# Holding the first store of a streaming RMSNorm until the fifth chunk has been loaded

## Chip, cores and metric

One core of one Trainium2 chip. The metric is the device time of one execution in microseconds (us), median over runs.

## The reference

```python
# x: (16, 1024, 512) float32, gamma: 512 ones, eps = 1e-5
rms = np.sqrt(np.mean(x ** 2, axis=-1, keepdims=True) + eps)
return np.maximum(x / rms * gamma, 0).astype(np.float32)
```

x has 33.55 MB, and the result as many: 67.1 MB must pass between HBM and the core whatever the schedule.

## The kernel before

The 16384 rows are cut into 8 chunks of 4.19 MB (128 partitions x 16 rows x 512 values). SBUF holds 6 chunks ("slots"). A chunk is normalised in place, and its slot is stored from where it was loaded. Every large transfer, load or store, is issued by SyncE into one queue. ScalarE squares and sums half a chunk at a time; VectorE follows with reciprocal, scaling and maximum, and counts each finished half chunk in `done`. GpSimd waits for each load and passes the news on to ScalarE.

```python
loads = [(0, 0, G), (0, G, K - G)] + [(i, 0, K) for i in range(1, nchunks)]   # chunk 0 in two halves
...
def store(i):
    nc.sync.dma_start(out=ov[i], in_=slot_ap(i)).then_inc(sem_slot[i % nslots], 16)
...
for m, (i, a, r) in enumerate(loads):
    if i < nslots:                        # chunks 0 to 5: issued at once
        load(m)
nxt = nslots
for i in range(nchunks):
    nc.sync.wait_ge(done, per * (i + 1))  # per = 2 half chunks
    store(i)
    if i >= 1 and nxt < nchunks:          # chunks 6 and 7 reuse slots 0 and 1
        nc.sync.wait_ge(sem_slot[nxt % nslots], 32)   # its load and its store have landed
        ... load(nxt); nxt += 1
```

`sem_slot[s]` rises by 16 when a load into slot s has landed and by 16 more when its store has.

Of the kernel before, what the change touches and what calls it, by code (L numbers as in the profile page):

```python
# [12 lines left out]
@with_exitstack  # L13
def kernel(
    ctx: ExitStack,
    tc: tile.TileContext,
    x: bass.AP,
    gamma: bass.AP,
    eps: bass.AP,
    out: bass.AP,  # L20
):



    nc = tc.nc
    P = nc.NUM_PARTITIONS

    x2 = x.flatten_outer_dims()
    out2 = out.flatten_outer_dims()
    n, d = x2.shape  # L30
    rows = n // P
    inv_d = 1.0 / d
    K = 16
    G = 8
    nchunks = rows // K
    nslots = 6
    ngroups = rows // G
    per = K // G
    xv = x2.rearrange("(c p k) d -> c p k d", p=P, k=K)
    ov = out2.rearrange("(c p k) d -> c p k d", p=P, k=K)  # L40

    singles = ctx.enter_context(tc.tile_pool(name="singles", bufs=1))
    psum = ctx.enter_context(
        tc.tile_pool(name="psum", bufs=1, space=bass.MemoryType.PSUM))

    gseed = singles.tile([P, d], F32, name="gseed")
    gamma_sb = singles.tile([P, d], F32, name="gamma_sb")
    eps_sb = singles.tile([P, 1], F32, name="eps_sb")
    ss = singles.tile([P, rows], F32, name="ss")
    rms = singles.tile([P, rows], F32, name="rms")  # L50
    rstd = singles.tile([P, rows], F32, name="rstd")
    slots = singles.tile([P, nslots * K * d], F32, name="slots")
    junk = psum.tile([P, G, d], F32, name="junk")


    loads = [(0, 0, G), (0, G, K - G)] + [(i, 0, K) for i in range(1, nchunks)]


    sem_half = tc.alloc_semaphore("half")
    sem_slot = [tc.alloc_semaphore(f"slot{s}") for s in range(nslots)]  # L60
    sem_g = tc.alloc_semaphore("gam")
    sem_z = tc.alloc_semaphore("zero")
    ready = tc.alloc_semaphore("ready")
    sq = tc.alloc_semaphore("sq")
    done = tc.alloc_semaphore("done")
    sa = tc.alloc_semaphore("sa")
    sv = tc.alloc_semaphore("sv")

    def slot_ap(i):
        s = (i % nslots) * K * d  # L70
        return slots[:, s:s + K * d].rearrange("p (k d) -> p k d", d=d)

    def load(m):
        i, a, r = loads[m]
        nc.sync.dma_start(out=slot_ap(i)[:, a:a + r, :],
                          in_=xv[i][:, a:a + r, :]
                          ).then_inc(sem_half if m == 0 else sem_slot[i % nslots], 16)

    def loaded(engine, m):
        i = loads[m][0]  # L80
        if m == 0:
            engine.wait_ge(sem_half, 16)
        else:
            engine.wait_ge(sem_slot[i % nslots], 32 * (i // nslots) + 16)

    def store(i):
        nc.sync.dma_start(out=ov[i], in_=slot_ap(i)).then_inc(sem_slot[i % nslots], 16)

    ctx.enter_context(tc.manual_schedule(engines={mybir.EngineType.SP}))
    with tc.tile_critical():  # L90
        for m, (i, a, r) in enumerate(loads):
            if i < nslots:
                load(m)
        nxt = nslots
        for i in range(nchunks):
            nc.sync.wait_ge(done, per * (i + 1))
            store(i)
            if i >= 1 and nxt < nchunks:
                nc.sync.wait_ge(sem_slot[nxt % nslots], 32)
                for m, (c, a, r) in enumerate(loads):  # L100
                    if c == nxt:
                        load(m)
                nxt += 1

        for m, (i, a, r) in enumerate(loads):
            loaded(nc.gpsimd, m)
            nc.gpsimd.sem_inc(ready, r // G)

        nc.vector.memset(gseed, 0.0).then_inc(sem_z, 1)  # L109
        nc.vector.memset(eps_sb, eps).then_inc(sem_z, 1)  # L110

        nc.scalar.wait_ge(sem_z, 1)
        nc.scalar.dma_start(out=gseed[0:P:32, :],
                            in_=gamma[None, :].to_broadcast([P // 32, d])
                            ).then_inc(sem_g, 16)
        nc.scalar.preload_act_table(ACTF.Sqrt)  # L116
        nc.scalar.wait_ge(sem_z, 2)
        with nc.scalar.Fori(0, ngroups) as gi:
            nc.scalar.wait_ge(ready, 1)
            nc.scalar.sem_inc(ready, -1)  # L120
            base = nc.scalar.snap((gi % (nslots * per)) * (G * d))
            col = nc.scalar.snap(gi * G)
            for j in range(G):
                a = nc.scalar.activation(  # L124
                    out=junk[:, j, :], in_=slots[:, bass.ds(base + j * d, d)],
                    func=ACTF.Square, accum_out=ss[:, bass.ds(col + j, 1)])
                if j == G - 1:
                    a.then_inc(sa, 1)
            nc.scalar.wait_ge(sa, 1)
            nc.scalar.sem_inc(sa, -1)  # L130
            nc.scalar.activation(out=rms[:, bass.ds(col, G)], in_=ss[:, bass.ds(col, G)],  # L131
                                 func=ACTF.Sqrt, bias=eps_sb, scale=inv_d).then_inc(sq, 1)

        nc.vector.wait_ge(sem_g, 16)
        nc.vector.stream_shuffle(gamma_sb, gseed, [0] * 32)  # L135
        with nc.vector.Fori(0, ngroups) as gi:
            nc.vector.wait_ge(sq, 1)
            nc.vector.sem_inc(sq, -1)  # L138
            base = nc.vector.snap((gi % (nslots * per)) * (G * d))
            col = nc.vector.snap(gi * G)  # L140
            blk = slots[:, bass.ds(base, G * d)]
            nc.vector.reciprocal(out=rstd[:, bass.ds(col, G)],  # L142
                                 in_=rms[:, bass.ds(col, G)]).then_inc(sv, 1)
            nc.vector.wait_ge(sv, 1)
            nc.vector.sem_inc(sv, -1)  # L145
            for j in range(G):
                row = slots[:, bass.ds(base + j * d, d)]
                r = nc.vector.scalar_tensor_tensor(  # L148
                    out=row, in0=row, scalar=rstd[:, bass.ds(col + j, 1)], in1=gamma_sb,
                    op0=ALU.mult, op1=ALU.mult)  # L150
                if j == G - 1:
                    r.then_inc(sv, 1)
            nc.vector.wait_ge(sv, 1)
            nc.vector.sem_inc(sv, -1)  # L154
            nc.vector.tensor_scalar_max(out=blk, in0=blk, scalar1=0.0).then_inc(done, 1)  # L155

    with nc.sync.register("landed") as landed:
        nc.sync.reg_mov(landed, 32)
        for s in range(nchunks - nslots, nslots):
            nc.sync.wait_ge(sem_slot[s], landed)  # L160
        nc.sync.reg_mov(landed, 64)
        for s in range(nchunks - nslots):
            nc.sync.wait_ge(sem_slot[s], landed)
# [35 lines left out]
```

## Time and profile before

| | before |
|---|---|
| time, median of the first 3 runs | 162.84 us (162.69 to 162.90) |
| span of the profiled run | 160.9 us |
| moved | 67.12 MB, mean 417 GB/s |
| busiest compute engine | VectorE, 78% |
| bulk queue, share of the 16 DMA engines' time | 97.6% |
| first store issued, landed | 31.07, 72.1 us |
| last VectorE instruction ends, last store lands | 146.4, 159.9 us |

The row to read is the DMA row, not the compute rows: engines with 54 and 78% wait for something. The page's chain of the last work ends at VectorE's last instruction, so what fills the last 13 us has to be looked up in SyncE's waits and in the transfers' landings. In lines of the profile, SPq is SyncE's sequencer, DVE is VectorE, ACT ScalarE and POOL GpSimd. In what follows L4 is the load and S4 the store of chunk 4, counted from 0, so that the "fifth chunk" is chunk 4.

### The profile page before, as it was taken

The page shows a single profiled execution, that of the slowest core. Times are in us where ns is not written, and L with a number is a line of the kernel's source. Part 1 is how long each engine was busy: PE and PEld are TensorE (multiplying, and loading weights), DVE is VectorE, ACT ScalarE, POOL GpSimd, SP SyncE. Part 2 cuts the span into 40 slices and gives each one's busy share as a digit, 9 for nine tenths or more (in the row PEclk, how much of TensorE's full clock was granted, in tenths as well). Part 3 has the DMA queues.
Part 4 walks back from the last instruction along what each step waited for, and adds up shares of the span by engine and source line. Part 5 has one row for each costly group of instructions (what it writes and reads, how often), then busy time and mean ns, then how long its engine had stood idle before and what let it go on. Part 6 is the DMA issues. An engine that isn't in the chain of part 4 may idle for free. (4 is left out here: it accounts for less than half of the span.)

```text
span 160.9 us, 1006 instructions
## 1 busy us (share of the span) xinstructions
DVE 126.0 (78%) x164; ACT 86.3 (54%) x273; POOL 0.2 (0%) x4
## 2 busy tenths in 40 slices
DVE  1103989898989899999999999999999999994000
ACT  3088929889988988988900198503994000000000
POOL 0000000000000000000000000000000000000000
DMA  5999999999999998999999999999999999999993
GB/s 155 434 432 415 521 391 391 513 399 391 489 424 391 481 432 367 415 391 489 424 391 489 424 391 448 464 391 440 456 407 432 456 415 424 464 415 424 464 407 138
DMA packets 2456, 67.12 MB, mean 417 GB/s; under 512 B 276, under 2 KB 276, under 8 KB 280
## 3 DMA queue, kind: packets, MB, share of 16 engines
q1 hardware_dynamic: 2448, 67.11, 97.6%
q10 hardware_dynamic: 8, 0.01, 0.0%
HBM read 33.56 MB, written 33.55 MB: 417 GB/s over the span
## 5 line engine op out<-in xcount | busy, mean ns | idle before, releaser
L124 ACT ACTIVATE junk<-slots 128x512 f32 x128 | 74.5, 582 | 30.6 <-ACTq L120 30.3
L148 DVE SCALAR_TENSOR_TENSOR slots<-slots,rstd,gamma_sb 128x512 f32 x128 | 86.2, 747 | 4.8 <-DVEq L145 4.8
L155 DVE TENSOR_SCALAR slots<-slots x16 | 36.7, 2294 | 2.4 <-DVEq L154 0.2
L124 ACT ACTIVATION_READ_ACCUMULATOR junk<-slots x128 | 23.9, 187 | 0.0
L142 DVE RECIPROCAL rstd<-rms x16 | 3.1, 196 | 6.3 <-DVEq L138 6.3
L131 ACT ACTIVATE rms<-ss,eps_sb x16 | 4.8, 301 | 3.0 <-ACTq L130 3.0
L135 DVE LOAD_MASK_SELECT gamma_sb<-gseed x1 | 0.0, 14 | 5.8 <-DMA gseed<-in_gamma_dram 5.8
L116 ACT ACT_TABLE_LOAD x1 | 1.3, 1283 | 2.8 <-issue 2.8
L109 DVE MEMSET gseed<- 128x512 f32 x1 | 0.5, 485 | 1.1 <-SPq L90 1.1
L135 DVE STREAM_SHUFFLE gamma_sb<-gseed 128x512 f32<-128x512 f32 x1 | 0.7, 715 | 0.0
L180 POOL MEMSET const-bfloat16-1.0<- 128x1 bf16 x1 | 0.1, 103 | 0.0
L180 POOL MEMSET const-uint8-127<- 128x1 uint8 x1 | 0.1, 102 | 0.0
L180 POOL MEMSET const-float32-0.0<- 128x1 f32 x1 | 0.1, 100 | 0.2 <-issue 0.2
L180 POOL MEMSET const-float32-1.0<- 128x1 f32 x1 | 0.1, 99 | 0.0
L110 DVE MEMSET eps_sb<- 128x1 f32 x1 | 0.1, 59 | 0.0
## 6 DMA issues: line engine op xcount, KB each, us to landing
out_dram<-slots SPq DMA_DIRECT2D x8, 4096.0 KB, 31.3
slots<-in_x_dram SPq DMA_DIRECT2D x7, 4096.0 KB, 30.3
slots<-in_x_dram SPq DMA_DIRECT2D x2, 2048.0 KB, 9.6
gseed<-in_gamma_dram ACTq DMA_DIRECT2D x1, 8.0 KB
```

What stands on the lines that cost most here:

```text
L109: nc.vector.memset(gseed, 0.0).then_inc(sem_z, 1)
L110: nc.vector.memset(eps_sb, eps).then_inc(sem_z, 1)
L116: nc.scalar.preload_act_table(ACTF.Sqrt)
L124: a = nc.scalar.activation(out=junk[:, j, :], in_=slots[:, bass.ds(base + j * d, d)], func=ACTF.Square, accum_out=ss[:, bass.ds(col + j, 1)])
L131: nc.scalar.activation(out=rms[:, bass.ds(col, G)], in_=ss[:, bass.ds(col, G)], func=ACTF.Sqrt, bias=eps_sb, scale=inv_d).then_inc(sq, 1)
L135: nc.vector.stream_shuffle(gamma_sb, gseed, [0] * 32)
L142: nc.vector.reciprocal(out=rstd[:, bass.ds(col, G)], in_=rms[:, bass.ds(col, G)]).then_inc(sv, 1)
L148: r = nc.vector.scalar_tensor_tensor(out=row, in0=row, scalar=rstd[:, bass.ds(col + j, 1)], in1=gamma_sb, op0=ALU.mult, op1=ALU.mult)
L155: nc.vector.tensor_scalar_max(out=blk, in0=blk, scalar1=0.0).then_inc(done, 1)
L180: nc = _bacc.Bacc("TRN2", target_bir_lowering=False, num_devices=1)
```

## The change

The first store is ready at 31 us, while four of the six early loads are still to land. The intent can be read as: let the loads go first and start storing only when most of the input is in.

```diff
         for i in range(nchunks):
             nc.sync.wait_ge(done, per * (i + 1))
+            if i == 0:
+                nc.sync.wait_ge(sem_slot[nslots - 2], 16)
             store(i)
```

## The prediction

> **What bounds the kernel now.** I began with the first two parts of the page, since a change of one wait in the DMA queue can only matter if that queue or what it feeds sets the end.
>
> ```profile
> DVE 126.0 (78%) x164; ACT 86.3 (54%) x273; POOL 0.2 (0%) x4
> DMA  5999999999999998999999999999999999999993
> q1 hardware_dynamic: 2448, 67.11, 97.6%
> ```
>
> No compute engine is full; the 16 DMA engines are, from the second slice to the last but one, and all bulk traffic is on one queue, q1, filled by SyncE. The chain that ended last is no help: it names one VectorE instruction ending at 146.4 us (144.14 + 2.29) of a 160.9 us span. The last 14 us are a transfer, so I read the queue's own waits next.
>
> ```profile
> SPq L87 <- DVE slots L155: 105.2, 6, 26.5
> SPq L75 <- DMA out_dram<-slots: 33.0, 2, 24.2
> SPq L163 <- DMA out_dram<-slots: 12.4, 1, 12.4
> ```
>
> L87 issues a store, L75 a load; the columns are total us, times and the longest. SyncE waits for most of the span, which looks like an idle transfer path. It is not: SyncE only hands out work, and the question is whether the engines run out of it. The stretches of one chunk's length (9.7 us), columns length, busy of DVE, ACT and POOL, clock, DMA share and GB/s, answer that:
>
> ```profile
> 32.00:41.70 9.70, 9.25 (x14) 8.75 (x29) 0.00 (x0) 1.00 1.00 432
> 41.70:51.40 9.70, 9.25 (x14) 9.23 (x31) 0.00 (x0) 1.00 1.00 432
> 51.40:61.10 9.70, 9.25 (x13) 8.75 (x30) 0.00 (x0) 1.00 1.00 402
> 61.10:70.80 9.70, 9.11 (x12) 8.75 (x30) 0.00 (x0) 1.00 1.00 432
> 148.40:158.10 9.70, 0.00 (x0) 0.00 (x0) 0.00 (x0) 1.00 1.00 432
> ```
>
> The DMA share is 1.00 while SyncE waits. (GB/s counts a packet in the stretch where it falls, so 402 with a share of 1.00 is counting, not a pause.) Last, the queue's own issues in order of time:
>
> ```profile
> 0.94 3.60 SPq L75 DMA_DIRECT2D slots<-in_x_dram  x7
> 31.07 16.83 SPq L87 DMA_DIRECT2D out_dram<-slots  x2
> 72.13 0.34 SPq L75 DMA_DIRECT2D slots<-in_x_dram  x1
> 72.51 0.73 SPq L87 DMA_DIRECT2D out_dram<-slots  x1
> 82.05 0.34 SPq L75 DMA_DIRECT2D slots<-in_x_dram  x1
> 82.44 64.36 SPq L87 DMA_DIRECT2D out_dram<-slots  x5
> ```
>
> All seven loads of chunks 0 to 5 are queued by 4.54 us. The first store goes in at 31.07 and the second at 47.56; the row merges them. Narrowing the window to one issue after another gives each one's time from issue to landing. For the last two early loads (issued at 3.59 and 4.10), then, from a second view, for the first store:
>
> ```profile
> DMA to landing us min/median/max: 48.5/53.4/58.3
> ```
>
> ```profile
> out_dram<-slots SPq DMA_DIRECT2D x1, 4096.0 KB, 41.0
> ```
>
> So the fifth load lands at 3.59 + 48.5 = 52.1 us, the sixth at 4.10 + 58.3 = 62.4, the first store at 31.07 + 41.0 = 72.1. Done likewise for the rest, with L for a load, S for a store and the chunk's number, the landings are L1 22.9, L2 32.6, L3 42.3, L4 52.1, L5 62.4, S0 72.1, S1 82.1, L6 91.4, S2 101.4, L7 111.0, S3 120.9, S4 130.7, S5 140.5, S6 150.2, S7 159.9. One chunk lands about every 9.7 us, in the order of issue. S0 spent 31.3 of its 41.0 us waiting behind loads.
>
> **What the Trainium skill says.** "DMA: Bandwidth & Descriptors", section "Queues, rings and completion order": on each of the 16 engines the descriptors of one queue are consumed in ring order. The landings agree: S0 sat in the ring from 31.07 on, yet L3, L4 and L5 came at the spacing of L2. The same page, "Why a DMA increments its semaphore by 16 and not by 1": only the full 16 means all landed. The new wait asks for 16 on the slot of chunk 4, which before its store gets only that one load, so it passes when the slowest engine has finished L4, at 52.1, and is no race. Its section "Where 436 GB/s comes from" puts the ceiling at 435.2 GB/s; the trace has 432, so only less traffic or fewer gaps could gain. "Perfetto Trace Analysis", "DMA Instruction — HWDGE (DVE, Sync)": the profiled slice of a DMA instruction does not contain the data movement. Here a store's issue is 0.34 us and its 4 MB take 9.7, so I count landings, not issues.
>
> **The change part by part.** Comparing the two programs' order shows that SyncE gets one wait more and that every engine keeps all its instructions in the old order. No byte, packet or arithmetic instruction is added or removed.
>
> *The wait itself.* S0 is ready at 31.07 (the first chunk's rows are done) and will be held to 52.1, so it is issued 21.1 us later, at about 52.2.
>
> *What follows on SyncE.* S1 was ready at 47.56. It now queues right behind S0, one issue of 0.34 us later, so about 52.6: 5.0 us later. Next SyncE waits for S0's landing before it issues L6.
>
> *Does the queue run dry?* When SyncE wakes at 52.1, L5 is still to be moved, and it lands at 62.4. The margin is 62.4 - 52.1 = 10.3 us, against 0.34 us for an issue. So S0 joins the ring some 10 us before its turn. The order L5, S0, S1 is what it was, so S0 still lands at 72.1, S1 at 82.1, and L6 (72.13) and L7 (82.05) are issued when they were. Cost on the path: 0.
>
> *ScalarE and VectorE.* The first loads they need are untouched until L6. It lands at 91.4; ScalarE, which has been waiting for it, needs about 6 us for the first half of a chunk (8 x 582 ns and 8 x 187 ns from the page's groups at most), so VectorE could take up chunk 6 at about 97. It comes to it only at 113.49, when it has finished chunk 5 and S5 is issued. That leaves 16 us to spare; for L7 (111.0 + 6 against 129.97) 13 us. VectorE's own end, 146.4, and so the issue of S7, stay, 3.7 us before S6 lands.
>
> *The sum.* 16 chunk transfers of 9.7 us are 155.2 us; the start takes 159.9 - 155.2 = 4.7; closing takes 160.9 - 159.9 = 1.0; the median outside the span is 162.84 - 160.9 = 1.9. None changes: 155.2 + 4.7 + 1.0 + 1.9 = 162.8 us.
>
> **The rivals.** First, that an early store already runs beside the loads, and holding it loses that overlap. For it speaks that S0 is queued 31 us before its turn. Against it, L3 to L5 would then be spaced wider than L1 to L2, and the share of 1.00 leaves nothing to overlap. If it were true, up to two chunks' worth of early store traffic (the 21 us) could shift to the end; even a half of that, 10 us, would make 173 us.
>
> Second, that the queue drains: the wake-up comes after the ring is empty. A wait for the sixth load instead would do this, and would cost an issue plus the first bytes' way. The first load shows that way: issued at 0.94, its 2 MB at 432 GB/s need 4.9 us, and it landed at 8.3, so about 2.5 us. That would make about 165.5 us, 1.6% slower. The 10.3 us of margin speak against it.
>
> Third, a gain: loads free of store traffic run faster, so chunks land sooner. But the loads before 62.4 already have the engines to themselves, at 432 GB/s both before and after S0 was queued. If queueing a store ahead cost each of L3 to L5 as much as 0.1 us, the gain is 0.3 us: 162.5.
>
> Fourth, the load of chunk 6 is released later and starves VectorE. That needs S0 to land later than 72.1 by more than the spare 13 to 16 us, and nothing makes it later at all.
>
> **Range and chances.** The three runs of before lie within 0.21 us, and nothing on the path moves, so the width is that of repeat runs and of another chip: 162.3 to 163.4. I give 0.98 to within 2%; 0.01 to slower, for an ordering in the ring that I misread; 0.01 to faster.
>
> **What would show it.** In the changed profile the first two stores should be issued at about 52.2 and 52.6 in one pair. SyncE's wait for S0 before L6 should shrink from 24.2 to about 19 us (from 53 to 72.1), and the total of that row from 33.0 to about 28. The latencies of S0 and S1 become 72.1 - 52.2 = 19.9 and 82.1 - 52.6 = 29.5; with the other six as they were (28.9, 38.5, 33.7, 27.0, 20.2, 13.4) the median store falls from 31.3 to about 28 us, which would be no gain, only less queueing. L6 should still be issued near 72.1, the last VectorE instruction end near 146.4, and the DMA share stay 9 in every inner slice. I am wrong if a slice near 52 to 75 us drops, if L6 is issued more than 1 us off 72.1, or if L3 to L5 land at another spacing than 9.7 us.

## The result, and the profile after

The changed kernel took 162.82 us (median of 6 runs, 162.68 to 163.11), before 162.84 (6 runs, 162.69 to 162.93). The ratio is 1.0002, 95% interval 0.9989 to 1.0015: no difference. Ratios here and below are the mean time of one kernel's fast runs over that of the other's of the same rounds, so not quite the ratio of the medians quoted.

The queue's issues in order of time, changed kernel (start us, us, engine, line, operation, count):

```profile
0.94 3.62 SPq L75 DMA_DIRECT2D slots<-in_x_dram  x7
52.18 0.82 SPq L87 DMA_DIRECT2D out_dram<-slots  x2
72.07 0.34 SPq L75 DMA_DIRECT2D slots<-in_x_dram  x1
72.45 0.68 SPq L87 DMA_DIRECT2D out_dram<-slots  x1
82.05 0.34 SPq L75 DMA_DIRECT2D slots<-in_x_dram  x1
82.43 64.38 SPq L87 DMA_DIRECT2D out_dram<-slots  x5
```

Only the second row differs from before by more than 0.1 us. The first two stores leave SyncE as a pair at 52.18 us instead of singly from 31.07 on. The next event that depends on a store's landing, the load of chunk 6, is issued at 72.07 (72.13 before), the load of chunk 7 at 82.05 (the same). What SyncE waited for in the changed kernel (total us, times, longest):

```profile
SPq L87 <- DVE slots L157: 62.6, 4, 16.1
SPq L98 <- DMA slots<-in_x_dram: 47.5, 1, 47.5
SPq L75 <- DMA out_dram<-slots: 28.0, 2, 19.1
```

L98 is the new wait. The waits were renamed and shifted. Two waits of 26.5 and 16.1 us for VectorE have become one of 47.5 for a load, and the wait for the first store's landing fell from 24.2 to 19.1 us, because SyncE begins it later. In the totals, L87 fell by 42.6 and L75 by 5.0, and 47.5 came in as L98: the account closes at 0.1 us. These are the waits of the engine that hands out work. What the engines that do the work show, from the page of the changed kernel:

```profile
DVE 126.0 (78%) x164; ACT 86.3 (54%) x273; POOL 0.2 (0%) x4
DMA  5999999999999998999999999999999999999993
q1 hardware_dynamic: 2448, 67.11, 97.5%
out_dram<-slots SPq DMA_DIRECT2D x8, 4096.0 KB, 28.1
```

The last row is the only one that looks like a gain: the median store takes 28.1 us from issue to landing, and took 31.3 before. It is queueing time. The first store landed 19.9 us after its issue instead of 41.0, having been issued 21.1 us later: 52.18 + 19.9 = 72.1, where it landed before.

### The profile page after: what moved, and what is told of

It reads as the page before. It is cut to its first block, busy times and chain, and to the rows that moved or that the text cites. A ratio compares the mean times of both kernels' runs of the same rounds, so it can differ in the third digit from the quotient of the medians.

```text
span 161.1 us, 1007 instructions
## 1 busy us (share of the span) xinstructions
DVE 126.0 (78%) x164; ACT 86.3 (54%) x273; POOL 0.2 (0%) x4
## 5 line engine op out<-in xcount | busy, mean ns | idle before, releaser
L126 ACT ACTIVATION_READ_ACCUMULATOR junk<-slots x128 | 23.9, 187 | 0.0
## 6 DMA issues: line engine op xcount, KB each, us to landing
out_dram<-slots SPq DMA_DIRECT2D x8, 4096.0 KB, 28.1
```

The lines of the kernel that those rows point to most:

```text
L126: a = nc.scalar.activation(out=junk[:, j, :], in_=slots[:, bass.ds(base + j * d, d)], func=ACTF.Square, accum_out=ss[:, bass.ds(col + j, 1)])
```

## The experiments

Theory A: a hold costs nothing as long as something is left in the DMA queue when the held store arrives, and past that point the hold costs its full length plus a restart. The main rivals are that the hold costs or gains in proportion to its length; that idle time early is caught up later; and that the result is null only because the store was stuck behind loads in one queue anyway. "Before" was run on the same chip beside each set.

### Holding longer: four lengths

Each is the changed kernel with another event in the new wait.

```diff
-                nc.sync.wait_ge(sem_slot[nslots - 2], 16)
+                nc.sync.wait_ge(done, 5)                     # e9_hold_558
+                nc.sync.wait_ge(sem_slot[nslots - 1], 16)    # e1_hold_sixth
+                nc.sync.wait_ge(done, 6)                     # e10_hold_64
+                nc.sync.wait_ge(done, 8)                     # e2_hold_chunk3
```

Expected of e9_hold_558: 

> The first store is held until VectorE has finished five half chunks, 55.8 us: 3.6 us later than the change does it, still some 6 us before the queue runs dry. Theory A (no cost as long as work is left in the queue): 162.5 to 163.2 us. If the cost grew with the time held from the start: by the two longer holds, in proportion to the hold beyond 31.07 (21.2 us at 49.5 us of hold), 10.6 us more, 173.4.

Expected of e1_hold_sixth: 

> The hold is moved from the fifth load to the sixth, so the first store is issued only at 62.4 us, when the last queued load has landed and nothing is left in the queue. Theory A (a hold costs nothing only as long as work is left in the queue; the margin of the change was 10.3 us): the queue runs dry and the start of a transfer, some 2.5 us by the estimate from the first load, comes on top: first store lands at about 74.6 instead of 72.1, and everything after it is shifted; time 164.5 to 165.5 us. Theory B (how long a store is queued ahead never matters at this size): 162.8.

Expected of e10_hold_64: 

> Held until six half chunks are done, 64.0 us: 2.0 us past the hold on the sixth load (issued at 61.96, time 165.32). Theory A with slope 1 past the dry point: 165.3 + 2.1 = 167.4 us, range 167.0 to 167.8; and the same restart cost as the holds to 61.96 and 80.55.

Expected of e2_hold_chunk3: 

> The first store is held until VectorE has finished the fourth chunk, 80.5 us. Theory A: the queue is empty from 62.4 on, so the gap is 80.5 - 62.4 = 18.1 us plus the start of about 2.5; 162.8 + 20.6 = 183.4 us, range 181 to 184. If a hold were absorbed later (theory C: the later stores are waiting for VectorE anyway, which ends at 146.4, so idle time early is caught up): clearly less than 181, down to about 165.

| first store issued | kernel | time, median us | ratio to before, 95% interval |
|---|---|---|---|
| 31.07 | before | 162.8 | 1 |
| 52.18 | the change | 162.82 | 1.0002 (0.9989 to 1.0015) |
| 55.79 | e9_hold_558 | 162.76 | 0.9991 (0.9971 to 1.0012) |
| 61.96 | e1_hold_sixth | 165.32 | 1.0159 (1.0145 to 1.0172) |
| 64.17 | e10_hold_64 | 167.60 | 1.0292 (1.0271 to 1.0313) |
| 80.55 | e2_hold_chunk3 | 183.96 | 1.1307 (1.1291 to 1.1324) |

All four came out inside their ranges, and the table has a knee. Up to 55.79 us a hold is free. Past 61.96 each microsecond held costs a microsecond: (before took 162.78 us on both of the chips that these three ran on) from e1 to e10 the issue moves by 2.2 us and the time by 2.3, from e1 to e2 by 18.6 and 18.6. Carried back from these three runs, the line of slope 1 meets 162.78 us at a hold to about 59.4 us (for e1, 61.96 - 2.54). So the cost may begin there, some 2.5 us before L5 lands, or jump later; no run between 55.79 and 61.96 tells. The cost is not proportional to the hold from its start (that would have given 173 for e9), and nothing is caught up. In stretches of e2_hold_chunk3 (length, busy of DVE, ACT, POOL, clock, DMA share, GB/s) the second row is most of the cost:

```profile
52.00:61.50 9.50, 9.05 (x12) 8.88 (x28) 0.00 (x0) 1.00 0.90 386
61.50:80.50 19.00, 17.96 (x23) 17.39 (x58) 0.00 (x0) 1.00 0.00 0
```

For 19 us the DMA engines moved nothing, while VectorE worked at 95% and ScalarE at 92%. The compute rows show no fault; the DMA row does.

The holds past the dry point also show the restart. Of the issues of e1_hold_sixth, then of e2_hold_chunk3, the held stores and the two loads after them (the rows between are left out):

```profile
61.96 0.82 SPq L87 DMA_DIRECT2D out_dram<-slots  x2
73.11 0.34 SPq L75 DMA_DIRECT2D slots<-in_x_dram  x1
83.81 0.34 SPq L75 DMA_DIRECT2D slots<-in_x_dram  x1
```

```profile
80.55 0.82 SPq L87 DMA_DIRECT2D out_dram<-slots  x2
91.69 0.34 SPq L75 DMA_DIRECT2D slots<-in_x_dram  x1
102.42 0.34 SPq L75 DMA_DIRECT2D slots<-in_x_dram  x1
```

The first load row is issued when S0 lands, the second when S1 does. On an empty queue S0 needs 11.1 us from issue to landing in both (as in e10), where a chunk in an unbroken stream takes 9.7: the start costs 1.4 us. S1 then takes 10.7 us in both, against 9.9 before. The full cost of e1, 165.32 - 162.78 = 2.5 us, is therefore not the start alone. The trace shows where the rest went. Two stretches of e1_hold_sixth, in which S1 and L6 are moved:

```profile
73.50:83.20 9.70, 9.25 (x14) 6.83 (x22) 0.00 (x0) 1.00 1.05 412
83.20:92.90 9.70, 9.25 (x13) 0.00 (x0) 0.00 (x0) 1.00 1.01 399
```

The engines are busy, and yet below the 432 GB/s of an unbroken stream: their packets (32 KB on one engine) took longer. Share x 16 x 32.77 KB over the rate gives a mean of 1.34 and 1.33 us for one, against 1.21 at 432. By the trace's records of single packets, the slow ones start at 81.1 to 83.0 and at 90.4 to 92.4 us, where S1 turns to L6 and L6 to S2, and cost 1.7 us together (mean of the 16 engines). The kernel before has its slow packets at the end of L5, where L5 turns to S0 (58.5 to 60.2 us, 0.7 us), and e1 has none there. Over the span, e1 has 1.4 us more of idle engines and 1.15 us more of slow packets than before, and the two spans differ by 2.6 (163.5 and 160.9). Why packets are slow at these places the runs do not settle.

### Moving the store forward in the same queue

```diff
-            if i < nslots:
+            if i < 4:
                 load(m)
 ...
             store(i)
+            if i == 0:
+                for m, (c, a, r) in enumerate(loads):
+                    if c in (4, 5):
+                        load(m)
```

> The loads of chunks 4 and 5 are issued after the first store, at 31.07 us, so the store goes 19.4 us earlier through the same queue, with load 3 still in it. Theory A (only the total of bytes and an unbroken queue count, the place of the store does not): store 0 lands at about 52.0, load 4 at 61.7, load 5 at 71.4; time 162.5 to 163.1. Rival (loads must go first, or reads and writes in another order have another rate): outside 162.3 to 163.4.

Measured: 163.06 us, ratio 1.0023 (1.0011 to 1.0035), before 162.78. The issues:

```profile
31.05 0.34 SPq L87 DMA_DIRECT2D out_dram<-slots  x1
31.44 0.91 SPq L75 DMA_DIRECT2D slots<-in_x_dram  x2
...
53.31 0.33 SPq L75 DMA_DIRECT2D slots<-in_x_dram  x1
```

S0 landed at 53.3, 19 us earlier than before, and nothing was gained. (S0, L4 and L5 landed at 53.3, 62.7 and 72.5, each 1.0 to 1.3 us later than expected.) So an early landing of S0, which lets the load of chunk 6 be issued 19 us earlier, is worth nothing. The time is inside the range of theory A, yet slower by 0.2%, outside the noise; the last set below takes this up.

### Taking the store out of the queue, with and without the hold

In the change S0 sits behind L5 either way, so the hold never moves its transfer. Here S0 goes through GpSimd's queue, with a semaphore `st0` of its own; SyncE leaves S0 out, and the waits on slot 0 are counted accordingly (not shown).

```diff
         for m, (i, a, r) in enumerate(loads):
             loaded(nc.gpsimd, m)
             nc.gpsimd.sem_inc(ready, r // G)
+            if i == 2:                                  # e6_own_queue_held: i == 4
+                nc.gpsimd.wait_ge(done, per)
+                nc.gpsimd.dma_start(out=ov[0], in_=slot_ap(0)).then_inc(st0, 16)
```

Expected without the hold: 

> The first store goes through GpSimd's own queue, issued after the third load has landed (32.6 us), its rows being done at 31.07. Now it need not stand behind the loads. If the two queues share the engines evenly: store 0 and load 3 both land near 52 (load 3 at 42.3 before), load 4 near 61.7, load 5 near 71.4. Theory A: the same bytes in an unbroken stream, time 162.4 to 163.4. Rival (an early store that runs beside loads uses capacity that loads alone leave idle): load 5 lands clearly before 71.4 and the time falls by over 1 us. Second rival (mixing reads and writes costs rate): time over 164.

Expected with the hold: 

> The same queue of its own, but the first store held until the fifth load has landed (52.1 us): the change under test, where the hold does move the transfer itself. Theory A: load 3 and load 4 land as before (42.3 and 52.1), store 0 and load 5 share and both land near 72; time 162.4 to 163.4, the same as the run without the hold. If holding an early store ever pays or costs where it is not stuck behind loads, this run and the one without the hold differ by more than 1 us.

Measured: 162.95 us without (ratio 1.0002, 0.9985 to 1.0020) and 162.79 with the hold (ratio 1.0000, 0.9983 to 1.0017), before 162.85. The store as GpSimd issued it, without the hold and then with it:

```profile
33.24 0.66 POOL L112 DMA_DIRECT2D out_dram<-slots  x1 [32.80 <-DMA slots<-in_x_dram]
```

```profile
52.79 0.66 POOL L112 DMA_DIRECT2D out_dram<-slots  x1 [52.35 <-DMA slots<-in_x_dram]
```

Issue to landing took 24.2 and 23.9 us, so S0 landed at 57.5 or 76.7. Its transfer did move by 19 us, and the time did not. L5 landed at 72.0 without the hold and at 67.0 with it. The expected landings were missed: without the hold L3 landed at 47.8, not 52, and S0 at 57.5; with it L5 at 67.0 and S0 at 76.7, not both at 72. The cause is a late start of the store, not an uneven share. Issued at 33.24, its first packet ran only at 38.6 us (with the hold at 57.8, issued at 52.79), and until then the loads had the engines alone. From 38.5 to 56 us without the hold, packets, MB and share of GpSimd's queue (q0) and SyncE's (q1):

```profile
q0 software_dynamic: 128, 4.19, 55.5%
q1 hardware_dynamic: 128, 3.67, 48.6%
```

The store moved 4.19 MB and the loads 3.67 MB, which is about even. The total stayed, which is what the theory is about.

### How much could a saving at this place give at all?

```diff
-            store(i)
+            if i == 0:      # wrong on purpose: one of the chunk's 16 rows per partition
+                nc.sync.dma_start(out=ov[0][:, 0:1, :],
+                                  in_=slot_ap(0)[:, 0:1, :]).then_inc(sem_slot[0], 16)
+            else:
+                store(i)
```

> Wrong on purpose: only one row in sixteen of the first chunk is stored, so 15/16 of 9.7 = 9.1 us of transfer are gone just where the change held a store. If the DMA engines alone set the end: 162.8 - 9.1 = 153.7 us. If the last store's issue, which waits for VectorE (146.46 us), is the next bound: the queue is dry before it, and it lands at 146.46 + 2.5 + 9.7 = 158.7; time about 161.6, range 160.3 to 162. The second is what I expect: a gain in the early store stage has a ceiling of 1 to 3 us.

Measured: 160.44 us (result wrong, as meant), ratio 0.9860 (0.9846 to 0.9874). Of 9.1 us of transfer taken away, only 2.3 came off the time. That is inside the expected range. A stretch near the run's end tells where the rest went, and the last issue:

```profile
140.00:145.00 5.00, 4.85 (x8) 0.00 (x0) 0.00 (x0) 1.00 0.00 0
```

```profile
144.16 2.29 DVE L159 TENSOR_SCALAR slots<-slots  x1
146.48 0.33 SPq L87 DMA_DIRECT2D out_dram<-slots  x1
```

From 140 to 145 us the DMA engines started nothing. The last store could go only when VectorE was done (144.16 + 2.29 = 146.45), was issued at 146.48, and needed 11.1 us on an empty queue, so it landed at 157.6, not at 158.7. VectorE is the second bound, close behind the first: any change to the early stores of this kernel can win at most about 2.3 us, even one that makes 15/16 of a store vanish.

### The 0.2% of the store moved forward

The run with the store ahead changes from loading to storing 4 times in the course of the queue, the kernel before 3 times. Two kernels varied that count with the queue kept full.

```diff
-            if i >= 1 and nxt < nchunks:          # e7_fewer_turns: L6, L7, then S2; 2 turns
+            while i == 1 and nxt < nchunks:
```

```diff
-            if i < nslots:                        # e8_more_turns: 4 loads, then store and load in turn; 5 turns
+            if i < 4:
                 load(m)
-        nxt = nslots
+        nxt = 4
 ...
-            if i >= 1 and nxt < nchunks:
-                nc.sync.wait_ge(sem_slot[nxt % nslots], 32)
+            if nxt < nchunks:
+                if nxt >= nslots:
+                    nc.sync.wait_ge(sem_slot[nxt % nslots], 32)
```

Expected of fewer turns: 

> The two late loads are issued one behind the other (6, 7), and the third store after both; same bytes, queue never dry. The queue then turns from loads to stores 2 times instead of 3. Theory T: each such turn costs about 0.35 us (in the traces so far the 15 whole chunks after the first take 1.1 us more than 15 x 9.707 with 3 turns, 1.54 us with the 4 turns of the run that puts the store ahead of two loads): 162.8 - 0.35 = 162.45 us, ratio 0.998. Rival: the extra of that run had another cause, and this one is equal to before, ratio 0.9995 to 1.0005.

Expected of more turns: 

> Four loads first, then store and load in turn (S0, L4, S1, L5, S2, L6, S3, L7, S4 ...): 5 turns from loads to stores instead of 3. Theory T: 162.8 + 2 x 0.36 = 163.5 us, ratio 1.0045. Rival: 162.8, or that of the run with the store ahead of two loads (ratio 1.0023) if only the first turn's place matters.

Measured: e7_fewer_turns 162.65 us, ratio 0.9984 (0.9969 to 1.0000); e8_more_turns 163.07 us, ratio 1.0012 (0.9995 to 1.0029); before 162.78. The first fits the theory of a price per turn, but its interval touches 1. The second misses: the expected 1.0045 lies outside its interval, and it is no slower than the run with 4 turns. In the traces' completion times the 15 whole chunks after chunk 0 take longer than 15 x 9.707 us by 0.95 us with 2 turns, 1.1 with 3, 1.54 with 4 and 1.84 with 5. That has the right direction, but it is one profiled run each; the change and e9_hold_558, also with 3 turns, have 1.2 each, and e8's profiled run was its slowest (163.51 us). The records of single packets speak against a price per turn. In the kernel before, the packets at the first turn are slow by 0.67 us (mean of the 16 engines), those at the other two by 0.03 in all; e7_fewer_turns has 0.71 at its first and nothing at its second, and the store moved forward 0.93 at its first and less than 0.1 at the other three. Only e8_more_turns, in its slow profiled run, has a second one: 1.03 at its first turn and 0.59 at its last. So the number of turns is not what counts; 0.26 us of what the store moved forward pays lies at its first turn, and the rest, and why that turn is slow, is open. No correct version here is clearly faster than both kernels.

## Why the prediction was right, by its own steps

- **The bound.** That the DMA engines' unbroken stream sets the end was shown by taking it apart: longer gaps cost just as much more (slope 1 past 61.96 us), and without 9.1 us of traffic the time fell until VectorE's last chunk set it.
- **Ring order and the landings.** S0 landed at 72.1 us with an issue at 31.07, 52.18 or 55.79 (the load that waits for it went out at 72.13, 72.07 and 72.02). This was the step on which everything rested. One reading on the way was wrong: the 402 GB/s from 51.4 to 61.1 us at a share of 1.00 are not counting, for no later stretch makes them up. The mean packet took 1.30 us there (1.00 x 16 x 32.77 KB over 402), because L5's last packets, with S0 next in the queue, are slow (up to 2.0 us each, 2.1 in the changed kernel). So L5 came 10.3 us after L4 before and 10.2 after the change, and the DMA row has an 8 near 62 us in both; the signs "9.7 us" for L5 and "9 in every inner slice" were not true of the kernel before either.
- **The wait itself.** Issue predicted at 52.2 and 52.6 in a pair, found at 52.18 in a pair. The row for S0's landing was predicted to shrink from 24.2 to about 19 and was 19.1; its total about 28, was 28.0; the median store about 28, was 28.1.
- **The margin.** Predicted 10.3 us. That was a little too much, because L5 lands later when a store follows it: 62.4 us before, but 4.11 + 57.8 = 61.9 in e1_hold_sixth, where nothing follows. To that landing the margin is 61.9 - 52.1 = 9.8 us. The holds to 55.79 (free) and 61.96 (not free) bracket it, and if the cost begins at 59.4, it is only 59.4 - 52.2 = 7.2 us.
- **The sum.** It had to come out at 162.8, since its 4.7 us for the start are what was left over. The start proper is 3.5 us (chunk 0 had landed whole at 13.2, and a chunk takes 9.7); the other 1.2 are spread over the 15 chunks after it, half of it at L5.
- **The drained queue as a rival.** Predicted about 165.5 for a hold on the sixth load; 165.32 measured. That was partly luck: the start on an empty queue is 1.4 us, not 2.5, and the rest of the cost lies in slow packets of the transfers after it.
- **The overlap as a rival.** Both runs with a queue of its own removed the ring order that the prediction had leaned on, and the time still did not move. The prediction named ring order as the reason that nothing is lost; the deeper one is that a stream without gaps moves the same bytes in the same time.
- **The gain as a rival.** A store that waits further back in the queue does not slow a load: L4 landed 48.5 us after its issue with the store queued from 31.07 on, and 48.5 without. Only L5, with the store right behind it, lands later, by 0.4 to 0.7 us against the three holds past 61.96, and those were slower in all.
- **The starved VectorE as a rival.** VectorE's busy time is 126.0 us in both, and the last store, which waits for its last instruction, is issued at 146.46 and 146.48.

## What to carry to other kernels

Before moving an issue in a DMA queue, ask how much work is left in it when the issue arrives: in this kernel, whose later work has time to spare, holding or hurrying a transfer while there was some changed its queueing time and the whole by 0.3 us at most (in the medians), and once there was none, every further microsecond of hold was paid in full. Long waits of the engine that issues, and shorter times from issue to landing, said nothing about the time while the DMA row was full. Take a suspected cost away altogether to see what the next bound leaves to be won.

## What the Trainium skill lacked or had wrong

- "DMA: Bandwidth & Descriptors", "Anatomy of one DMA", gives a fixed cost of about 2.0 us for the GpSimd path, and its "Latency and other measured facts" about 0.6 us to the first byte for SyncE's. The whole fixed cost, landing included, of a large store issued by SyncE on an empty queue is not there; the runs show 1.4 us over the 9.7 us of a 4.19 MB chunk (11.1 us from issue to landing, in four kernels), 0.8 us of it before the first packet.
- The same page, "Where 436 GB/s comes from", says that for transfers between HBM and SBUF the HBM side, about 358 GB/s, binds. This kernel, on one core, held 432 GB/s in loads and stores alike; "HBM Reference", "Specifications (TRN2)", has it right that a core alone goes well above its share.
- The same page's "Queues, rings and completion order" describes turns between queues at packet granularity, without a figure for what a load and a store then get of the engines. Here the turns were about even: 4.19 MB of the store and 3.67 MB of loads from 38.5 to 56 us. The figure of about 1 us to the first byte that "Latency and other measured facts" gives for GpSimd's path is too small here: the first packet of the store ran 5.3 and 5.0 us after its issue.
- No page read for this case says that a load lands later when a store is right behind it in the queue: L5 landed at 62.3 to 62.4 us with a whole store there, and at 61.7 to 61.9 with none; its last packets took up to 2.0 us instead of 1.21 in the kernel before.
